# Hymba decoder layer on one core: values and decayed keys turned by VectorE and a DRAM scratch, transfers that add, one reciprocal-root operation in the layer norms, and a new order

## The chip, the cores and the metric

The kernel runs on one core of a Trainium2 chip. The core has a matrix engine (TensorE, PE in the profile, with its weight loads as PEld), VectorE (DVE), ScalarE (ACT), GpSimd (POOL) and SyncE (SP), which work in parallel, each through its own list of instructions in order, and which wait for each other by semaphores. SBUF is the memory on chip with 128 partitions, PSUM holds matmul results, DRAM lies outside and is reached by DMA transfers that an engine issues on its queue. The metric is the device time of one execution in microseconds (us), lower is better.

## The reference

One layer of a hybrid decoder, for a prompt of 512 tokens and, beside it, 8 decode tokens with their own past. All in float32, model width 1024.

```
h = x @ w_in                       # 3600 columns: qa ka va za ga | qb kb vb gb
# mixer A: gated linear attention, 4 heads, dk 64, dv 128, chunks of 64 tokens
S_t = diag(a_t) S_{t-1} + k_t^T v_t ;  o_t = q_t S_t        # a_t from za
o_a = rms_norm(o_a) * g
# mixer B: 8 heads of 64; three dilated windows (128,1) (512,4) (2048,16) with a
# relative-position bias, merged by their softmax denominators
mix = concat(o_a * silu(ga), o_b * silu(gb))
y   = mix @ w_out
out = layer_norm(alpha * x + y) * g + b                     # alpha = 2 ** 0.25
```

Outputs are the new rows of prompt and decode tokens, the GLA states (the prompt's last one, and s*a + k*v for each decode token), and the new key and value rows.

## The kernel before

**Tiling.** Everything is unrolled. The 512 prompt tokens and 8 decode tokens are projected in two halves (264 and 256 columns, the decode tokens in the first). Each fp32 product is three matmuls: weights and inputs are split into a high and a low part. `dense` (L804) holds the backbone of TensorE in the order of `ORDER` (L82): 21 groups of weight columns, qa0 to ga3, and then the output projection. For values (vb, va) the first half of the tokens comes out with features on partitions, and has to be turned to have tokens there; the second half is made in token layout at once.

**What sets the order.** `Plan` (L198) is a list scheduler that runs at build time. Each stage is a generator that yields operations, added with `add(gen, prio)`; the planner always takes the operation that can start first by its own cost table, the lower priority number first among equals, and issues it on its engine. Buffers come from `SLOTS` (SBUF, by tag) and `BANKS` (PSUM). So one engine's instruction order is fixed when the kernel is built, and every priority, slot count and cost moves it. All planned operations have the line of the helper that issues them, L380 in the profile.

**What is turned, and how.** `turn` (L730) copies a piece of 128 features by 256 tokens out of PSUM and turns it with two PE transposes (`ps_turn`); `vb_into` (L1219) uses it for the values of mixer B, f = 0 and 1 for each of v0 and v1. `gla_state` (L1019) turns the decayed keys `kd` (2 x 128 x 512) with eight PE transposes into `ps_kt` and copies them to `kt`, which the products `ps_kv` use. The output projection's pieces of tokens 0 to 255, in `out_turn` (L785), go another way for three of four column groups g: `blocks` (L740) turns 32 x 32 blocks on VectorE into `yw`, `store_blocks` writes `yw` to the DRAM scratch `ysc`, and `load_turned` loads it as `yx`, both on POOL's queue (`QUEUE`, y = "G"). `out_evac` (L1827) then adds `yx` to `y` with the residual's ALPHA, and takes `bn_stats`. The fourth group is turned by PE (`ps_yt`).

**The decode states.** `sample_state` (L1522) loads eight states `s` and their values `v`, multiplies by the decay on ScalarE, adds value times key on VectorE (16 operations each) and stores.

**Layer norm and end.** `norm` (L1874) centres each tile t of 128 tokens and scales it by a root from Ln and Exp with a Newton step (`rsqrt`, L410). Tile 3 ends the kernel: `early_mean` (L1698) prepares its mean, the last 256 columns are accumulated last in PSUM onto a seed that ScalarE writes, and `last_norm` (L1721) finishes: square and sum (`sq_y`), root, centre, three scalings and three stores. `ln_rows` (L1663) does the decode rows (`w_s`, `sums_s`), with two tiny products `ps_ms` and `ps_vs` that stand in PE's list among the last groups.

## Time and profile before

| | us |
|---|---|
| median of three runs | 276.61 (276.04 to 276.85) |
| the profiled execution | 276.23 |
| its span | 274.3 |
| busy: TensorE / VectorE / ScalarE / POOL | 264.2 / 220.6 / 157.9 / 64.0 |

The span reaches from the first to the last instruction of the profiled execution, which itself took 1.93 us more. The trace gives each instruction's start and duration; "<-" after idle time names what ended it. Names are the program's tiles, such as `ps_kt<-cf,kd` for a matmul into `ps_kt` from `cf` and `kd`. PE's own time is pipelined: a matmul of 256 columns is listed with 0.28 us, but the next one starts 0.12 after it.

### The profile page before, as it was taken

What the parts mean: (1) busy time and instruction counts of PE and PEld (TensorE: products, weight loads), DVE (VectorE), ACT (ScalarE), POOL (GpSimd) and SP (SyncE); (2) the same over time, 40 slices, a digit from 0 to 9 for tenths busy, and PEclk for the clock granted to TensorE, in tenths of its full rate; (3) what the DMA queues carried; (4) which work ended last, traced back from release to release, by engine and by line L of the source; (5) the groups of instructions that cost most, each with busy time, mean ns of one, the idle gap of its engine ahead of it and who ended that gap; (6) DMA issues with size and microseconds to landing.
All of it is one profiled execution on the core that took longest, in us unless ns stands there. A gap on an engine that the chain in (4) does not pass through costs nothing.

```text
span 274.3 us, 7448 instructions
## 1 busy us (share of the span) xinstructions
PE 264.2 (96%) x2869; PEld 248.9 (91%) x2869; DVE 220.6 (80%) x584; ACT 157.9 (58%) x478; POOL 64.0 (23%) x77
## 2 busy tenths in 40 slices
PE   8999999999799999999999999999999999999990
PEld 5999999899799999989998989999999999998890
DVE  5746789998989799988499954965989898448995
ACT  4727856565457676686464754735589975420221
POOL 3000000000576538220054435353200001330000
PEclk9999999999999999999999999999999999999997
DMA  6978948327959968737599999897952485896142
GB/s 212 342 192 196 301 130 226 81 76 210 307 172 278 236 206 273 194 84 203 153 223 279 282 219 272 217 206 162 244 159 76 114 290 144 228 282 192 58 171 81
DMA packets 62999, 54.67 MB, mean 199 GB/s; under 512 B 13933, under 2 KB 55059, under 8 KB 62965
## 3 DMA queue, kind: packets, MB, share of 16 engines
q1 hardware_dynamic: 61909, 52.18, 69.4%
q0 software_dynamic: 480, 1.57, 2.2%
q8 instruction: 22, 0.36, 0.5%
q10 hardware_dynamic: 576, 0.46, 0.5%
q14 instruction: 12, 0.10, 0.1%
HBM read 47.26 MB, written 7.73 MB: 200 GB/s over the span
## 4 chain that ended last, share of the span: by engine, by line
PE 80%; DMA 8%; DVE 6%; issue 2%; SPq 1%; POOL 0%; ACT 0%; DVEq 0%; POOLq 0%
PE ps_kb L380 9%; PE ps_ga L380 9%; PE ps_gb L380 9%; PE ps_qb L380 9%; PE ps_vb_f L380 4%; PE ps_va_f L380 4%; PE ps_vb L380 4%; PE ps_va L380 4%; PE ps_qa L380 4%; DMA ysc<-yw 4%; PE ps_yf L380 4%; DVE y L380 4%; PE ps_pv L380 3%; PE ps_s L380 3%; PE ps_ka L380 3%; DMA yx<-ysc 3%
## 5 line engine op out<-in xcount | busy, mean ns | idle before, releaser
L380 POOL TENSOR_TENSOR past<-past,qbc 128x256 f32<-128x256 f32 x32 | 29.0, 939 | 86.2 <-DMA qbc<-qsd 77.5
L380 POOL TENSOR_TENSOR vv<-vv,pb 128x256 f32<-128x256 f32 x32 | 26.8, 867 | 48.9 <-DMA pb<-psd_s 43.2
L380 ACT ACTIVATE pr<-pr,ms 128x128 f32<-128x128 f32 (+3 forms) x48 | 23.0, 493 | 7.8 <-DVE ms L380 7.8
L380 ACT COPY pt<-ps_pt 128x256 f32<-128x256 f32 (+1 forms) x29 | 9.8, 347 | 10.4 <-PE ps_pt L380 10.2
L380 DVE CUSTOM_DVE_ANT_0 pr<-ps_s,strip 128x128 f32<-128x128 f32 (+3 forms) x32 | 11.5, 407 | 3.9 <-PE ps_s L380 3.8
L380 ACT ACTIVATE sg<-sg 128x264 f32<-128x264 f32 (+1 forms) x32 | 13.7, 429 | 0.6
L380 PE MATMUL ps_ka<-xx,hi_ka 128*128 128x264 f32 (+1 forms) x64 | 12.2, 283 | 0.0
L380 POOL DMA_DIRECT2D ysc<-yw x3 | 2.5, 818 | 41.0 <-DVE yw L380 40.6
L380 PE MATMUL ps_pt<-cf,pr 128*128 128x128 f32 x56 | 11.3, 274 | 0.0
L380 DVE TENSOR_REDUCE lt<-past 128x8 f32<-128x512 f32 x16 | 10.5, 668 | 0.0
L380 PEld LDWEIGHTS ps_ka<-xx,hi_ka 128*128 128x128 f32 x64 | 9.9, 190 | 0.1
L380 DVE TENSOR_REDUCE o_pv<-vv 128x4 f32<-128x1024 f32 x8 | 9.7, 1206 | 0.0
L380 ACT ACTIVATE d<-d 128x512 f32<-128x512 f32 x11 | 6.6, 641 | 3.9 <-DVE d L380 3.8
L380 PE MATMUL ps_ka<-xx,lo_ka 128*128 128x264 f32 (+1 forms) x32 | 8.7, 283 | 0.0
L380 ACT ACTIVATE qh<-ps_qb 128x128 fp32r<-128x128 f32 x16 | 5.2, 438 | 5.9 <-PE ps_qb L380 5.8
L380 ACT COPY feat_y<-ps_yf 128x256 f32<-128x256 f32 x8 | 3.0, 373 | 8.9 <-PE ps_yf L380 8.9
L380 DVE TENSOR_TENSOR far<-tp,same 128x128 f32<-128x128 f32 (+1 forms) x16 | 8.1, 526 | 0.0
L380 DVE STREAM_TRANSPOSE yw<-feat_y 128x256 f32<-128x256 f32 x6 | 3.8, 640 | 4.8 <-ACT feat_y L380 4.7
L380 PE MATMUL ps_qa<-xx,hi_ka 128*128 128x264 f32 (+1 forms) x32 | 7.4, 304 | 0.1
L380 ACT CAST mhb<-gb 128x256 fp32r<-128x256 f32 x8 | 3.2, 405 | 7.2 <-DVE gb L380 7.2
L380 PEld LDWEIGHTS ps_pt<-cf,pr 128*128 128x128 f32 x56 | 6.9, 140 | 0.3 <-ACT hi_gb__2144 L380 0.2
L380 DVE TENSOR_TENSOR gb<-ps_gb,sg 128x256 f32<-128x256 f32 x8 | 3.4, 419 | 4.4 <-ACT sg L380 4.1
(574 smaller groups left out, 1079.1 us busy)
## 6 DMA issues: line engine op xcount, KB each, us to landing
past<-in_ck_dram SPq DMA_DIRECT2D x8, 512.0 KB, 4.7
vv<-in_cv_dram SPq DMA_DIRECT2D x8, 512.0 KB, 7.2
pb<-psd_s SPq DMA_DIRECT2D x16, 256.0 KB, 7.1
s<-in_state_dram SPq DMA_DIRECT2D x4, 512.0 KB
qbc<-qsd SPq DMA_DIRECT2D x8, 256.0 KB, 5.4
y<-in_xp_dram SPq DMA_DIRECT2D x4, 512.0 KB
x_raw<-in_xT_dram SPq DMA_DIRECT2D x6, 260.0 KB, 5.9
out_dram<-y SPq DMA_DIRECT2D x3, 512.0 KB
```

The lines of the kernel that those rows point to most:

```text
L380: getattr(eng.eng, op.fn)(*op.args, **op.kw)
```

## The change

1. Values of mixer B are turned by `blocks` on VectorE and a scratch `vsc` on SyncE's queue (new `rows_of`), the decayed keys by `blocks` and a scratch `ksc` on POOL's queue, in place of PE transposes.
2. Of the decode states, ScalarE multiplies both parts; the decayed state is stored plainly and the key times value is added to it in DRAM by an accumulating transfer.
3. The residual of tiles 0 and 1 is scaled by ALPHA on ScalarE after loading, and the projection's pieces are added to it by accumulating transfers from `ysc`; the statistics wait for each.
4. The layer norm roots are one Abs_reciprocal_sqrt with the Newton step as before; tile 2's mean and variance are made on ScalarE; in `last_norm` the centring stands ahead of the root; two of the last three stores go to SyncE's queue.
5. One slot of `w` more and one of `sv` less; `va1` ahead of `gb3`; nearly all priorities renumbered.

```diff
-SLOTS = dict(g=23, w=7, r=3, sv=5, pt=2, ...
+SLOTS = dict(g=23, w=8, r=3, sv=4, pt=2, ...
-QUEUE = dict(y="G")
+QUEUE = dict(y="G", v="D", k="G")
-ORDER = "... gb1 va0 gb2 gb3 va1 ga0 ga1 ga2 ga3".split()
+ORDER = "... gb1 va0 gb2 va1 gb3 ga0 ga1 ga2 ga3".split()
...
         if between:
-            yield S.activation(o, x, AF.Ln, scale=scale, bias=ln_eps)
+            yield S.activation(o, x, AF.Abs_reciprocal_sqrt, scale=scale, bias=ln_eps)
             yield V.tensor_scalar(half, x, -0.5 * scale, -0.5 * eps, op0=ALU.mult, op1=ALU.add)
-            yield S.activation(o, o, AF.Exp, scale=-0.5)
...
+    def rows_of(g, f, ps):
+        yield from make(f"vbw{g}", Need("g", f"vbw{g}", [P, 2, 2, P])) if f == 0 else iter((At(f"vbw{g}"),))
+        w = B[f"vbw{g}"]
+        feat = yield Need("t1", "feat", [P, GW])
+        yield copy(feat, ps[:, :GW])
+        free(ps)
+        yield blocks(w[:, :, f], feat)
+        free(feat)
+        if f:
+            yield store_blocks(queue["v"], vsc[g], w.rearrange("p t f c -> p (t f) c"))
+            free(w)
+            yield load_turned(queue["v"], B[f"v{g}"][:, :2, :].rearrange("p t (k j) -> p (t k) j", j=32), vsc[g])
...
+        kx = yield Need("g", "kx", [P, 2, NP])
+        for m in range(2):
+            yield blocks(kx[:, m].rearrange("p (c t) -> p c t", c=TT), kd[:, m])
+        yield store_blocks(queue["k"], ksc, kx.rearrange("p m (c t) -> p (m c) t", c=TT))
         kt = yield Need("g", "kt", [P, 2, TT, P])
-        for m in range(2):
-            ps = yield bank("t", "ps_kt")
-            for c in range(TT):
-                yield T.transpose(ps[:, c * P:c * P + P], kd[:, m, c * P:c * P + P], ident)
-            yield copy(kt[:, m].rearrange("p c t -> p (c t)"), ps)
+        yield load_turned(queue["k"], kt.rearrange("p m c (a j) -> p (m c a) j", j=32), ksc)
...
-            ps, raw = yield from turn(ps)
-            free(raw)
-            yield copy(B[f"v{i}"][:, :2, f * P:f * P + P], ps[:, :GW].rearrange("p (t c) -> p t c", t=2))
+            yield from rows_of(i, f, ps)
...
-                    yield S.mul(s4[:, bb, m, :], s4[:, bb, m, :], a_s[:, m, bi:bi + 1])
-                    yield V.scalar_tensor_tensor(s4[:, bb, m, :], v4[:, bb, m, :], ka_s[:, m, bi:bi + 1], s4[:, bb, m, :],
-                                                 op0=ALU.mult, op1=ALU.add)
+            for x, scale in ((s4, a_s), (v4, ka_s)):
...
+                yield D.dma_start(to, x) if scale is a_s else G.dma_start(to, x, accum_op=ALU.add)
...
+        if t < 2:
+            yield S.mul(y, y, ALPHA)
...
         yield At("early_centre")
-        yield S.activation(root, ss, AF.Ln, scale=1.0 / DM, bias=q)
+        yield V.scalar_tensor_tensor(y[:, x], ps, mean, B["gamma"][:, x], op0=ALU.subtract, op1=ALU.mult)
+        yield S.activation(root, ss, AF.Abs_reciprocal_sqrt, scale=1.0 / DM, bias=q)
         yield V.tensor_scalar(half, ss, -0.5 / DM, dev, op0=ALU.mult, op1=ALU.add)
-        yield V.scalar_tensor_tensor(y[:, x], ps, mean, B["gamma"][:, x], op0=ALU.subtract, op1=ALU.mult)
-        yield S.activation(root, root, AF.Exp, scale=-0.5)
...
-            yield (D if i == 1 else S).dma_start(y_p[t * P:t * P + P, c], y[:, c])
+            yield (D if i else S).dma_start(y_p[t * P:t * P + P, c], y[:, c])
...
-            yx = yield Need("g", f"yx{g}", [P, 2, GW])
-            yield load_turned(queue["y"], yx.rearrange("p t (k j) -> p (t k) j", j=32), ysc[g])
             for t in range(2):
-                add(out_evac(t, g, yx[:, t]), 2)
+                yield At(f"y{t}")
+                yield G.dma_start(B["y", t][:, g * GW:g * GW + GW].rearrange("p (k j) -> p k j", j=32),
+                                  ysc[g][8 * t:8 * t + 8].rearrange("k p j -> p k j"), accum_op=ALU.add)
+                add(out_stats(t, g, 1), 9.2)
...
+            sq = yield Need("r", f"sq{t}", [P, DM])
+            yield S.activation(sq, y, AF.Identity, accum_out=mv[:, 0:1])
+            yield S.mul(mean, mv[:, 0:1], -1.0 / DM)
+            yield S.activation(sq, y, AF.Square, bias=mean, accum_out=mv[:, 1:2])
```

What this does to the instruction lists is shown at three places. The first is TensorE's list before, inside the third part of the values group vb0 (`ps_vb0_3`, from weights `hi0_vb0`, `lo0_vb0` and inputs `xx`), with `ps_pt21` a transpose of the attention and `ps_kt` the turned keys:

```order
L380 MATMUL ps_vb0_3_1538<-hi0_vb0__912,xx0_133 128x256
L380 MATMUL ps_pt21_1524<-cf_66,pr20_1331 128x128 x2
L380 MATMUL ps_vb0_3_1538<-hi0_vb0__912,xx2_215 128x256
L380 MATMUL ps_vb0_3_1538<-lo0_vb0__991,xx2_215 128x256
L380 MATMUL ps_vb0_3_1538<-hi0_vb0__912,xx2_216 128x256
L380 MATMUL ps_kt_1532<-cf_66,kd_1408 128x128 x4
```

The same part of the same group in the changed kernel, on TensorE:

```order
L382 MATMUL ps_vb0_3_1539<-hi0_vb0__909,xx0_132 128x256
L382 MATMUL ps_vb0_3_1539<-lo0_vb0__910,xx0_132 128x256
L382 MATMUL ps_vb0_3_1539<-hi0_vb0__909,xx0_133 128x256
L382 MATMUL ps_vb0_3_1539<-hi0_vb0__909,xx2_215 128x256
L382 MATMUL ps_vb0_3_1539<-lo0_vb0__910,xx2_215 128x256
L382 MATMUL ps_vb0_3_1539<-hi0_vb0__909,xx2_216 128x256
```

The four transposes of the keys are gone from the list, as are the second four and those of the values, and nothing takes their place.

The second is the end of POOL's list, which issues the scratch transfers of the projection's pieces; before:

```order
L380 DMA ysc0_95<-yw0_3878 128x4x128
L380 DMA ysc1_96<-yw1_3921 128x4x128
L380 DMA yx0_3918<-ysc0_95 128x16x32
L380 DMA ysc2_97<-yw2_3957 128x4x128
L380 DMA yx1_3953<-ysc1_96 128x16x32
L380 DMA yx2_4004<-ysc2_97 128x16x32
```

In the changed kernel, where `out_3_dram<-v40` and `<-v41` are the state adds and `y0`, `y1` the tiles that are added to:

```order
L382 DMA out_3_dram<-v40_3486 128x8x128
L382 DMA ysc0_95<-yw0_3875 128x4x128
L382 DMA ysc1_96<-yw1_3910 128x4x128
L382 DMA y0_3706<-ysc0_95 128x8x32
L382 DMA y1_3708<-ysc0_95 128x8x32
L382 DMA y0_3706<-ysc1_96 128x8x32
L382 DMA y1_3708<-ysc1_96 128x8x32
L382 DMA ysc2_97<-yw2_3952 128x4x128
L382 DMA out_3_dram<-v41_3813 128x8x128
L382 DMA y0_3706<-ysc2_97 128x8x32
L382 DMA y1_3708<-ysc2_97 128x8x32
```

The third store stood behind one load and stands behind four adds now, and a state add has come between it and the two adds that need it.

The third is VectorE's list in the last groups of the output projection, up to the copy of `ps_ms` and the first work that needs the third scratch; before:

```order
L380 BN_STATS stats1_3729<-y1_3728 128x6
L380 SCALAR_TENSOR_TENSOR y2_4042<-y2_4042,ps_y20_4079 128x512
L380 BN_STATS stats2_4043<-y2_4042 128x6 x2
L380 COPY sums_s_85<-ps_ms_4118 64x1
L380 TENSOR_SCALAR w_s_3730<-w_s_3730,sums_s_85 64x128
L380 SCALAR_TENSOR_TENSOR y0_3726<-y0_3726,yx2_4004 128x256
L380 SCALAR_TENSOR_TENSOR y1_3728<-y1_3728,yx2_4004 128x256
```

In the changed kernel the two statistics at the top are those that wait for the adds from the second scratch:

```order
L382 BN_STATS stats0_3707<-y0_3706 128x6
L382 BN_STATS stats1_3709<-y1_3708 128x6
L382 TENSOR_TENSOR y0_3706<-y0_3706,ps_yt3_4033 128x256
L382 TENSOR_TENSOR y1_3708<-y1_3708,ps_yt3_4033 128x256
L382 BN_STATS stats0_3707<-y0_3706 128x6
L382 BN_STATS stats1_3709<-y1_3708 128x6
L382 SCALAR_TENSOR_TENSOR w_s_3710<-w_s_3710,ps_ys_4076 64x128
L382 TENSOR_REDUCE sums_s_85<-w_s_3710 64x1
L382 SCALAR_TENSOR_TENSOR y2_4035<-y2_4035,ps_y20_4068 128x512
L382 COPY sums_s_85<-ps_ms_4105 64x1
```

The sums that `ps_ms` is made from stand behind those statistics; the additions of `yx` and tile 2's statistics are gone.

More of the change, by code (lines that the diff above doesn't have):

```diff
@@ L96, in __init__ @@
             self.writes.append(kw["accum_out"])
+        if "accum_op" in kw:
+            self.reads = self.reads + [aps[0]]
         if fn == "tensor_tensor_reduce":
@@ L408, in cst, with rsqrt @@
         return const.tile(shape, dt, name=name)
-    def rsqrt(o, x, scale, eps, between=None):
+    def rsqrt(o, x, scale, eps, between=None, late=False):
         n = size(x)
@@ L424, in rsqrt @@
             yield V.tensor_scalar(x, x, scale, eps, op0=ALU.mult, op1=ALU.add)
-            yield S.activation(o, x, AF.Ln)
-            yield S.activation(o, o, AF.Exp, scale=-0.5)
+            if late:
+                yield S.activation(o, x, AF.Abs_reciprocal_sqrt)
+            else:
+                yield S.activation(o, x, AF.Ln)
+                yield S.activation(o, o, AF.Exp, scale=-0.5)
             yield V.tensor_tensor(t, o, o, op=ALU.mult)
@@ L750, in load_turned @@
         return q.dma_start(out, sc.rearrange("k p j -> p k j"))
+    def rows_of(g, f, ps):
[10 more added lines that the diff above has]
+            yield load_turned(queue["v"], B[f"v{g}"][:, :2, :].rearrange("p t (k j) -> p (t k) j", j=32), vsc[g])
+            for _ in range(2):
+                mark(f"vb{g}")
     def sample_rows(x, rows):
@@ L832, in dense @@
         free(zw, *xraw)
-        add(gate_decay(pz), 19.1)
+        add(gate_decay(pz), 41.3)
         yield from make("ka", Need("g", "ka", [P, 2, NP]), 3)
@@ L843, in dense @@
             add(residual(t), 10.3)
-        add(residual_sample(), 19.7)
+        add(residual_sample(), 40.8)
         units = [(g, f) for g in range(4) for f in range(2)]
@@ L960, in gla_levels @@
             if li % 2:
-                add(gla_level(made), 46.7)
+                add(gla_level(made), 62.4)
                 made = []
@@ L1121, in gla_out @@
         for i in range(2):
-            add(gla_head(u, i, ps, po), 26 + u + i / 2)
+            add(gla_head(u, i, ps, po), 51.1 + u + i / 2)
     def gla_head(u, j, ps, po):
@@ L1163, in evac @@
             if n == "k":
-                add(keys_out(ps, m, u), 9.7)
+                add(keys_out(ps, m, u), 56.4)
             else:
@@ L1772, in out_first @@
             yield from out_half(g, f, p, range(4, KT))
-            add(out_turn(g, f, p), 0.3)
+            add(out_turn(g, f, p), 10.7)
     def out_half(g, f, ps, ks):
@@ L1830, in out_evac, with out_stats @@
         c = slice(g * GW, g * GW + size(ps))
-        yield V.scalar_tensor_tensor(y[:, c], y[:, c], ALPHA, ps, op0=ALU.mult, op1=ALU.add)
+        if t < 2:
+            yield V.tensor_tensor(y[:, c], y[:, c], ps, op=ALU.add)
+        else:
+            yield V.scalar_tensor_tensor(y[:, c], y[:, c], ALPHA, ps, op0=ALU.mult, op1=ALU.add)
         free(ps)
-        for i in range(g, g + size(ps) // GW):
-            yield V.bn_stats(st[:, i, :], y[:, i * GW:i * GW + GW])
+        yield from out_stats(t, g, size(ps) // GW)
+    def out_stats(t, g, n):
+        y, st = B["y", t], B["stats", t]
+        for i in range(g, g + n):
+            if t not in (2,):
+                yield V.bn_stats(st[:, i, :], y[:, i * GW:i * GW + GW])
             mark(f"y{t}_done")
@@ L1867, in residual_sample @@
         free(ps, avg)
-        yield from rsqrt(rstd, sums[:, 1:2], 1.0, LN_EPS)
+        yield from rsqrt(rstd, sums[:, 1:2], 1.0, LN_EPS, late=True)
         yield V.scalar_tensor_tensor(y, y, rstd, gamma, op0=ALU.mult, op1=ALU.mult)
```

99 lines of the change are left out of this document (51 added, 48 removed).

## The prediction

> **What bounds the kernel now.** I read the page's header first: busy time of each engine, the row of tenths, the software queue and the chain that ended last.
>
> ```profile
> span 274.3 us, 7448 instructions
> PE 264.2 (96%) x2869; PEld 248.9 (91%) x2869; DVE 220.6 (80%) x584; ACT 157.9 (58%) x478; POOL 64.0 (23%) x77
> PE   8999999999799999999999999999999999999990
> q0 software_dynamic: 480, 1.57, 2.2%
> PE 80%; DMA 8%; DVE 6%; issue 2%; SPq 1%; POOL 0%; ACT 0%; DVEq 0%; POOLq 0%
> ```
>
> TensorE is busy in 39 of 40 slices, so what it no longer does comes off the end, unless another chain ends as late. The next view cuts the span into stretches: start and end, length, then the busy time of PE, PEld, DVE, ACT and POOL, the granted clock, the DMA share and GB/s.
>
> ```profile
> 60.00:100.00 40.00, 38.53 (x583) 36.46 (x583) 35.69 (x92) 25.12 (x72) 18.72 (x20) 1.00 0.78 220
> 245.00:267.60 22.60, 22.60 (x126) 19.21 (x124) 20.49 (x60) 3.73 (x20) 1.15 (x1) 1.00 0.46 152
> 267.60:274.30 6.70, 0.01 (x1) 0.00 (x0) 3.35 (x9) 1.06 (x4) 0.00 (x0) 0.76 0.24 83
> ```
>
> PE has no gap from 245 on, and VectorE is nearly as full there (20.49 of 22.60). After 267.6 only the last layer norm and its stores are left. So two chains meet at the end: PE's, and the one that feeds VectorE with the projection pieces of tokens 0 to 255, which go through a DRAM scratch on the POOL queue. The timeline of POOL (start, duration, what) shows the second; the last two lines are the chain's, where a duration reaches to the landing.
>
> ```profile
> 232.41 0.93 POOL L380 DMA_DIRECT2D ysc<-yw  x1 [38.61 <-DVE yw L380]
> 238.04 1.17 POOL L380 DMA_DIRECT2D yx<-ysc  x1 [1.97 <-DMA ysc<-yw]
> 239.67 0.76 POOL L380 DMA_DIRECT2D ysc<-yw  x1 [0.47 <-DVE s L380]
> 240.42 1.16 POOL L380 DMA_DIRECT2D yx<-ysc  x1
> 239.67 5.38 DMA ysc<-yw
> 245.59 7.09 DMA yx<-ysc
> 252.70 0.76 DVE L380 SCALAR_TENSOR_TENSOR y<-y,yx 128x256 f32<-128x256 f32 x2 [0.53 <-DMA yx<-ysc]
> 253.37 0.75 DVE L380 BATCH_NORM_STATS2 stats<-y 128x6 f32<-128x256 f32 x2
> 254.52 2.47 DVE L380 SCALAR_TENSOR_TENSOR y<-y,mv,gamma 128x1024 f32<-128x1024 f32 x2
> ```
>
> The last of these loads is in at 252.70, and VectorE then works until 268.35 without a real pause, 15.65 us. PE's last matmul ends at 267.61 (below). The two are within 1 us, so a gain needs both. The profiled execution took 276.23 us, 1.93 more than its span; the sum is made against it. The median of the three runs is 276.61, 0.38 more.
>
> **PE's transposes.** Two edits take work from PE: the values of tokens 0 to 255 (four pieces, two transposes each) and the decayed keys (eight) are turned by VectorE and a DRAM scratch. The chain view gives start, duration and count:
>
> ```profile
> 85.05 0.22 PE ps_turn L380 x2
> 90.57 0.44 PE ps_kt L380 x4
> 93.26 0.44 PE ps_kt L380 x4
> 54.40 0.69 issue
> 73.62 1.47 issue
> ```
>
> Removed: 2 x 0.44 + 4 x 0.22 = **1.76 us** in a stretch without slack. The order of the changed kernel has no other matmul fewer or more. In their place VectorE gets block transposes:
>
> ```profile
> L380 DVE STREAM_TRANSPOSE yw<-feat_y 128x256 f32<-128x256 f32 x6 | 3.8, 640 | 4.8 <-ACT feat_y L380 4.7
> 93.87 1.72 DVE L380 TENSOR_TENSOR lo_kb__1590<-raw_kb__1078,hi_kb__1395 128x1024 fp32r<-128x1024 f32 x1
> 103.30 0.28 PE L380 MATMUL ps_kb<-xx,lo_kb__1590 128*128 128x264 f32 x1
> L380 PEld LDWEIGHTS ps_kv<-va,kt x64: 129/133/133, 189.1 to 194.1; 64*64 64x64 f32 x64
> ```
>
> Four of 0.64 for the values and two of twice the size, 1.28 each, for the keys: 5.1 us, of which 3.8 fall into the stretch 60 to 100, whose 35.69 become 39.5 of 40. That is the tightest place. What hides it is the lead of the weight splits: lo_kb__1590 is ready at 95.59 and first used at 103.30. The lead of 7.7 falls to some 4; without it each further us is one of PE. The turned keys are needed at 189.1, about 95 us after they were made, so a store and a load of 5 to 7 us each vanish there. They also put a wait on POOL (the load stands behind its store, ahead of the fifth past product), and POOL has time: 64.0 of 274.3 busy. The turned values come one scratch trip later, and the new order has moved the products that read them behind the next projection groups. Cost taken: 0, bounds 0 to 2 us. The two "issue" pauses (0.69 and 1.47, PE waiting for nothing that shows, behind bursts of small matmuls) stay, move or go: -2.2 to +1.5, taken as 0.
>
> **The sample state.** Sixteen VectorE operations go and sixteen ScalarE ones come:
>
> ```profile
> L380 DVE SCALAR_TENSOR_TENSOR s<-v,ka_s,s 128x128 f32<-128x128 f32 x16 | 5.0, 344 | 0.8 <-ACT s L380 0.8
> L380 ACT ACTIVATE s<-s,a_s 128x128 f32<-128x128 f32 x16 | 6.0, 408 | 0.0
> ```
>
> VectorE gains 5.0 us, ScalarE pays 16 x 0.408 = 6.5; it is busy 157.9 of 274.3, and no end waits for it there. The two new 512 KB adds into the output matter only as company on the POOL queue.
>
> **The y pieces.** Here lies the risk. Three loads of 256 KB become six adding transfers of 128 KB on the same queue, and POOL's order is new: four adds now stand ahead of the third store, and the second state add ahead of the last two. The six VectorE adds go.
>
> ```profile
> L380 DVE SCALAR_TENSOR_TENSOR y<-y,yx x6: 417/419/425, 244.3 to 253.0; 128x256 f32<-128x256 f32 x6
> DMA to landing us min/median/max: 5.8/6.2/7.1
> L380 PE MATMUL ps_ms<-sums_s,avg x2: 167/182/198, 250.8 to 250.9; 66*66 66x1 f32 x2
> ```
>
> Everything before comes 1.76 earlier, so the first adds are issued at 238.04 - 1.76 = 236.3, then about 1.0 apart (between 0.76 and 1.17 a DMA), the fourth at 239.3. The third store follows at 240.3 and lands after 5.38, at 245.7; 0.5 later the last two adds, at 246.2 and 247.2 (the state add is issued in that wait). With the median of 6.2 the last add lands at **L = 253.4**, 0.7 later than the load did. No row shows an adding transfer. From below: the queue's packets took 2.2% of 274.3 = 6.0 us for six transfers, 1.0 per 256 KB, so 0.5 per add if adding is free. From above: a store and a load behind each other, 5.38 + 7.09 = 12.5 us for one. I take the price of a load, since the rows of one are the nearest; the other end is the first rival.
>
> After L VectorE has less to do: of the 15.65, 0.76 (adds of y) and 0.75 (the statistics of tile 2, now on ScalarE) and 0.26 (their aggregate, by the same step) go, leaving 13.9; and tile 0's own add lands 1.0 ahead of tile 1's, so part of its 1.24 (half of 2.47) stands before L. I take 13.3. The chain then ends at 253.4 + 13.3 = 266.7 instead of 268.35. Two places of PE must also not wait: ps_ms, now 249.0, stands behind statistics that wait for the fourth add (239.3 + 6.2 = 245.5, and behind it five or six operations of about 0.42, some 2.3 us: 247.8, so 1.2 us of slack), and the last unit, whose seed stands on ScalarE behind the root chains of tiles 0 to 2 (it holds until L is about 255.7).
>
> A rule speaks against this. The Trainium skill, "Collectives: The Full Stack", section "The bandwidth ceiling: the fold count and why AG ≠ RS ≠ AR", says that a DMA that adds is slower not for the arithmetic but because it reads two sources on one ring, so that it moves about half as much. No run here shows it yet; by it an add would take 1.0 of the queue instead of 0.5, which the 1.0 between issues still covers, and the sum would be about 0.5 higher.
>
> **The layer norm roots.** One operation replaces Ln and Exp, and it needs another ACT table.
>
> ```profile
> 267.33 0.28 PE L380 MATMUL ps_y<-hi_wo__3598,mla 128*128 128x256 f32 x1
> 268.25 0.29 ACT L380 ACTIVATE tail<-tail,tail 128x1 f32<-128x1 f32 x1
> 268.57 0.20 ACT L380 ACTIVATE tail<-tail 128x1 f32<-128x1 f32 x1
> 268.65 0.47 DVE L380 SCALAR_TENSOR_TENSOR y<-ps_y,tail,gamma 128x256 f32<-128x256 f32 x1
> 270.10 1.41 ACTq L380 DMA_DIRECT2D out_dram<-y  x2
> 270.76 0.33 SPq L380 DMA_DIRECT2D out_dram<-y  x1
> L597 ACT ACT_TABLE_LOAD x1 | 1.3, 1283 | 1.7 <-PEq L2021 1.7
> 252.26 0.31 ACT L380 ACTIVATE sq_s<-w_s 64x128 f32<-64x128 f32 x1 [7.40 <-DVE w_s L380]
> ```
>
> At the end the Exp's step goes (0.20 and a gap of 0.03), and the centring of 0.47 runs beside the square instead of behind it; about 0.3 us. The last store, the second of two on ScalarE's queue (1.41 / 2 = 0.7), goes to SyncE's (0.33): another 0.3. Together **0.6**, between 0.2 and 1.0. The new table load stands behind sq_s, where ScalarE had waited 7.40 us and has only 3.73 us of work in 22.6. Its 1.283 is hidden if what comes next waits for L, as it does.
>
> The Trainium skill, "ScalarE: Activation LUTs", section "What ACT_TABLE_LOAD costs", adds a drain of about 1380 ns to the load of 1283 ns; the load agrees with the row, the drain no run here shows. By it 2.66 us would still lie inside that wait, and the sum is the same.
>
> **The sum.** PE: last matmul 267.61 - 1.76 = 265.85; behind it came 276.23 - 267.61 = 8.62, now 8.0: 273.9. VectorE: 266.7, and behind it 276.23 - 268.35 = 7.88, now 7.3: 274.0. The later is 274.0 against 276.23; the median would stand up to 0.38 higher, and I say **274.2**.
>
> **Rivals.**
> (a) *Adds that clog the queue: slower.* If an add occupies the queue for t us, then above t = 1.0 (the distance of the issues) the third store stands behind four of them and the last add behind one more: L = 253.4 + 0.5 + 5 (t - 1). The kernel is slower than before once L + 13.3 + 7.3 passes 276.23, L = 255.6, t about 1.35. At t = 2 L is 258.9 and the time **279.5**; the last unit of PE waits too, inside the same chain. For it: reading, adding and writing 128-byte rows in SBUF is nowhere in the trace, and the order puts the third store behind the adds. Against it: 0.5 us plain is 2.7 times below the turning point.
> (b) *The gain is spent elsewhere: no change.* A full VectorE at 60 to 100, a longer pause after the small matmuls, or the order's new places cost PE 1.5 to 2.5 us in the middle: **276**. For it: 39.5 of 40. Against: the lead of 7.7 us, and 5.0 us that VectorE is spared elsewhere.
> (c) *The pauses vanish with the new order*: 274.2 - 2.2 = **272.0**, if L also comes early.
> (d) *It does not do what it says*, the transposes gone but the y chain not shorter (L as late as 255): within 0.3% of before; I count it with (b).
>
> **How the numbers follow.** Forecast 0.58, (a) 0.23, (b) with (d) 0.14, (c) 0.05. Faster by over 0.3% (0.83 us, about what a measurement of this kernel can tell from no change): 0.58 + 0.05 = 0.63; same 0.14; slower 0.23. The forecast's own range is 272.8 to 275.6: terms of -0.4 and +0.4 in the tail, -1 for pauses, +1 for L. The range for 8 in 10 goes down to (c)'s 272.0 and up to 279.0, most of (a); beyond it lie about half of (a) and half of (c), 0.14.
>
> **What would show it.** Right: no ps_kt, PE's last matmul near 265.9; the last add of y landing at 253 to 254.5; the statistics of tile 0 not waiting past 253; a table load inside ScalarE's wait before the roots; the final stores in at 272 or earlier. Wrong: VectorE idle before statistics on an adding transfer past 255, PE idle before ps_ms or the last unit (case a); PE idle between 75 and 130 on a split of weights or on "issue" (case b); adds that take more than 1.35 us of the software queue each.

## The result: slower, and the profile after

The changed kernel takes **280.60 us** (median of four runs, 280.52 to 281.31) against 276.73 for the kernel before beside it: a ratio of **1.0139** (95% interval 1.0107 to 1.0171). The forecast was 274.2, with a range that ended at 279.0. So both the sign and the range were wrong, and the rival that had named this outcome, the adds that clog the queue, came in. The profiled execution took 281.31 us, 5.08 more than that of before.

The page's header, in the same order as before: busy times, the 40 slices of TensorE and of its granted clock, the software queue, and one group of instructions with what ended the idle time ahead of it.

```profile
span 279.5 us, 7413 instructions
PE 264.9 (95%) x2853; PEld 248.6 (89%) x2853; DVE 228.0 (82%) x580; ACT 159.4 (57%) x474; POOL 74.3 (27%) x84
PE   8999999999999989999999999999989999986990
PEclk9999999999999999999999999999999999997996
q0 software_dynamic: 8848, 3.67, 10.4%
L382 DVE BATCH_NORM_STATS2 stats<-y 128x6 f32<-128x256 f32 x11 | 4.5, 419 | 13.9 <-DMA y<-ysc 13.9
```

TensorE has 16 instructions fewer, as forecast, but is busy 0.7 us longer. Two slices near the end show holes: PE falls to 8 tenths in slice 36 and to 6 in slice 37, and the clock to 7 tenths in slice 37. VectorE stood idle 13.9 us in all ahead of the statistics of `y`, waiting for adding transfers. And the software queue has 8848 packets where it had 480, in 10.4% of the span instead of 2.2%.

The views by stretch (start and end, length, busy time of PE, PEld, DVE, ACT and POOL, granted clock, DMA share, GB/s):

```profile
60.00:100.00 40.00, 39.62 (x590) 38.18 (x589) 39.91 (x92) 23.53 (x71) 17.98 (x23) 1.00 0.80 236
245.00:267.60 22.60, 19.29 (x86) 15.38 (x84) 13.82 (x32) 7.57 (x22) 4.27 (x3) 0.92 0.92 139
250.50:253.80 3.30, 0.00 (x0) 0.02 (x1) 2.61 (x9) 0.00 (x0) 1.35 (x2) 1.00 1.27 174
253.80:257.80 4.00, 3.99 (x12) 3.21 (x13) 1.14 (x3) 1.69 (x3) 1.77 (x2) 0.58 1.20 74
```

From 245 on PE was full before (22.60 of 22.60) and VectorE nearly (20.49). Now both have holes: PE does nothing at all for 3.3 us, and then works for 4 us at a granted clock of 0.58.

The timelines of POOL, VectorE and PE (start, duration, engine, what; in brackets the idle time ahead and what ended it) give the chain behind these holes. The last two rows sum up the six adds: the duration of an issue on POOL (ns; shortest, median, longest) with the first and the last start, and the time from issue to landing.

```profile
236.13 3.21 POOL L382 DMA_DIRECT2D y<-ysc  x2
240.65 3.11 POOL L382 DMA_DIRECT2D y<-ysc  x2 [1.31 <-DMA ysc<-yw]
242.42 2.14 POOL L382 DMA_DIRECT2D ysc<-yw  x1
243.20 2.95 POOL L382 DMA_DIRECT2D out_dram<-v  x1
252.45 3.12 POOL L382 DMA_DIRECT2D y<-ysc  x2 [6.30 <-DMA ysc<-yw]
251.48 0.43 DVE L382 BATCH_NORM_STATS2 stats<-y 128x6 f32<-128x256 f32 x1 [0.66 <-DMA y<-ysc]
258.11 0.43 DVE L382 BATCH_NORM_STATS2 stats<-y 128x6 f32<-128x256 f32 x1 [3.13 <-DMA y<-ysc]
253.81 0.25 PE L382 MATMUL ps_ms<-sums_s,avg 66*66 66x1 f32 x2 [3.31 <-issue]
L382 POOL DMA_DIRECT2D y<-ysc x6: 1535/1928/2283, 236.1 to 253.3; - x6
DMA to landing us min/median/max: 5.3/9.8/12.3
```

The third store is issued at 242.42 and is in only at 252.45, ten us later, where a store took 5.38 before; behind it the last two adds begin. The first of them, tile 0's, lands at **L = 258.11**, and VectorE works on from there; the second, issued at 253.3 and 5.3 us under way, lands at about 258.6, before VectorE asks for it. The forecast for the last add was 253.4. The fourth add lands at 251.48 instead of 245.5, and since the sums for `ps_ms` stand behind its statistics in VectorE's list, PE waits 3.31 us there. The trace calls that wait "issue"; the release is read from VectorE's list, which reaches the sums (253.43 to 253.71) just ahead of it.

### The profile page after: what moved, and what is told of

It is laid out like the page before. It is cut to its first block, busy times and chain, and to the rows that moved or that the text cites. A ratio compares the mean times of both kernels' runs of the same rounds, so it can differ in the third digit from the quotient of the medians.

```text
span 279.5 us, 7413 instructions
## 1 busy us (share of the span) xinstructions
PE 264.9 (95%) x2853; PEld 248.6 (89%) x2853; DVE 228.0 (82%) x580; ACT 159.4 (57%) x474; POOL 74.3 (27%) x84
## 3 DMA queue, kind: packets, MB, share of 16 engines
q0 software_dynamic: 8848, 3.67, 10.4%
## 5 line engine op out<-in xcount | busy, mean ns | idle before, releaser
L382 POOL TENSOR_TENSOR past<-past,qbc 128x256 f32<-128x256 f32 x32 | 26.4, 859 | 82.3 <-DMA qbc<-qsd 80.0
L382 POOL TENSOR_TENSOR vv<-vv,pb 128x256 f32<-128x256 f32 x32 | 27.8, 897 | 56.9 <-DVE ms L382 20.3
L382 ACT ACTIVATE pr<-pr,ms 128x128 f32<-128x128 f32 (+3 forms) x48 | 22.7, 491 | 12.6 <-DVE ms L382 12.6
L382 DVE BATCH_NORM_STATS2 stats<-y 128x6 f32<-128x256 f32 x11 | 4.5, 419 | 13.9 <-DMA y<-ysc 13.9
L382 PE MATMUL ps_pt<-cf,pr 128*128 128x128 f32 x56 | 10.9, 276 | 1.0 <-ACT pt L382 0.6
L382 POOL DMA_DIRECT2D y<-ysc x6 | 9.4, 1910 | 7.6 <-DMA ysc<-yw 7.6
L382 ACT COPY pt<-ps_pt 128x256 f32<-128x256 f32 (+1 forms) x23 | 7.6, 348 | 5.7 <-PE ps_pt L382 5.6
L382 POOL DMA_DIRECT2D out_dram<-v x2 | 4.6, 2278 | 21.2 <-ACT v L382 21.2
L382 DVE TENSOR_SCALAR pr<-pr,ms 128x320 f32<-128x320 f32 (+3 forms) x16 | 7.9, 497 | 0.2
L382 DVE TENSOR_TENSOR far<-tp,same 128x128 f32<-128x128 f32 (+1 forms) x16 | 7.1, 475 | 0.0
L382 ACT CAST xx<-x_raw 128x520 fp32r<-128x520 f32 (+2 forms) x10 | 5.3, 540 | 3.0 <-DMA x_raw<-in_xT_dram 2.9
```

The lines of the kernel that those rows point to most:

```text
L382: getattr(eng.eng, op.fn)(*op.args, **op.kw)
```

## The experiments

All ratios are to the kernel before, measured on the same chip beside the run, with 95% intervals.

**Which of the adds costs it.** Three kernels put parts of the change back. `e1_y_plain` loads the projection's pieces plainly, three loads of 256 KB, and adds them on VectorE; all else is the changed kernel:

```diff
-            for t in range(2):
-                yield At(f"y{t}")
-                yield G.dma_start(B["y", t][...], ysc[g][...], accum_op=ALU.add)
-                add(out_stats(t, g, 1), 9.2)
+            yx = yield Need("g", f"yx{g}", [P, 2, GW])
+            yield load_turned(queue["y"], yx..., ysc[g])
+            for t in range(2):
+                add(out_evac(t, g, yx[:, t]), 9.2)
```

> The changed kernel with the projection pieces of tiles 0 and 1 loaded plainly from their scratch and added by VectorE, as before; the state adds stay on POOL's queue. Theory A (the six y adds clog the software queue): the load of the third piece lands at about 253 instead of 258.4, TensorE does not wait before ps_ms, its clock does not drop, its last matmul ends at about 267.6 and the time is 275.5 to 277. Rival B (the new order in the middle of the kernel sets the time): no more than 1 us comes back, 279.5 or more. Rival C (the state add of 512 KB on the same queue is as bad): the load lands at 255 or later, 278 to 279.

`e2_state_plain` has the adds for `y`, and the decode states as before (ScalarE's multiply, VectorE's multiply and add, one store):

> The changed kernel with the decode states added by VectorE and stored once, as before; the six y adds stay. Theory A: the queue still has six adds of about 2.3 us, the last lands near 255 because the third store now stands behind two of them fewer and the 4.2 us of the state add are gone: 277 to 278.5, still slower than before. Rival C (the state add is what delays the last y adds): the last add lands before 254 and the time is 276.5 or less. Rival B: 280, no change.

`e3_no_adds` has both edits:

> The changed kernel without any adding transfer: turned values and keys, new roots, new priorities stay. Theory A: 275 to 276, bounded by TensorE, whose list up to the last ps_yf ends at 244.3 in both kernels; so the 1.76 us of transposes stay lost in the middle and only the end gains. Rival B: 279 or more. Rival D (the adds were the only loss, the transposes' gain comes through without them): 274 or less.

| | median us | ratio |
|---|---|---|
| e1, y plain | 275.24 | 0.9952 (0.9932 to 0.9972) |
| e2, state plain | 280.48 | 1.0145 (1.0102 to 1.0189) |
| e3, neither adds | 276.36 | 0.9985 (0.9960 to 1.0011) |

The adds into `y` cost 5.2 us with the state's adds beside them (1.0139 - 0.9952 = 1.87% of 276.7) and 4.4 without (1.0145 - 0.9985 = 1.60%); they are the whole loss and more. Taking the state's adds out, which gives VectorE its sixteen operations back, gains nothing that shows; with plain loads of `y` they even seem to gain about 0.9 us (0.9952 against 0.9985, though the two intervals overlap a little). e2 missed its expectation of 277 to 278.5. In its trace the last add lands at 256.06, some 2.5 us earlier than in the changed kernel, but PE still waits 2.06 us at `ps_ms` and the clock is 0.57 for 4 us behind it; what keeps its time at 280.5 was not separated. The rest of the change is worth half a per cent, as e1 shows. In e1 the queue and the first work that needs the third scratch are:

```profile
q0 software_dynamic: 2848, 3.67, 6.7%
252.63 0.76 DVE L382 TENSOR_TENSOR y<-y,yx 128x256 f32<-128x256 f32 x2 [1.33 <-DMA yx<-ysc]
245.00:267.60 22.60, 21.94 (x123) 18.66 (x121) 19.86 (x57) 8.14 (x25) 1.17 (x1) 1.00 0.53 146
```

L is 252.63, the clock 1.00, and PE has 21.94 of 22.60 again.

**What of it is the adding, what the six transfers in that order.** `e9_six_loads` keeps the six transfers of 128 KB and their places in POOL's list, but loads and lets VectorE add:

```diff
-                yield G.dma_start(B["y", t][...], ysc[g][8 * t:8 * t + 8]..., accum_op=ALU.add)
-                add(out_stats(t, g, 1), 9.2)
+                yx = yield Need("g", f"yx{g}{t}", [P, GW])
+                yield G.dma_start(yx..., ysc[g][8 * t:8 * t + 8]...)
+                add(out_evac(t, g, yx), 9.2)
```

> The changed kernel with the same eleven transfers in the same order on POOL's queue, but the six of y are plain loads of 128 KB into six tiles, and VectorE adds them. If the adding itself holds the queue (1024 packets of 128 bytes, about 2 us an add): the last pair lands near 253 and the time is 275 to 276.5, as with three loads. If six transfers with the third store behind four of them are the cause, whatever they do: 279 or more.

`e5_rows_1k` adds in the same six places, but each transfer has 128 rows of 1 KB in DRAM and SBUF instead of 1024 pieces of 128 bytes. It leaves out the turn of these pieces, so tiles 0 and 1 get other values:

```diff
-                yield G.dma_start(B["y", t][...].rearrange("p (k j) -> p k j", j=32),
-                                  ysc[g][8 * t:8 * t + 8].rearrange("k p j -> p k j"), accum_op=ALU.add)
+                yield G.dma_start(B["y", t][...],
+                                  ysc[g][8 * t:8 * t + 8].rearrange("k (a b) j -> (k a) (b j)", b=8), accum_op=ALU.add)
```

> The changed kernel with the same six adds of 128 KB, but each reads its half of the scratch as 128 rows of 1 KB and not as 1024 pieces of 128 bytes: the pieces are added without their turn, so tiles 0 and 1 of the output are not the reference's. If an add costs by the packet (36 ns for 128 bytes and 64 ns for 512 in the changed kernel's queue, so some 100 ns for 1 KB, 0.8 us of 16 engines instead of 2.3), the adds no longer clog the queue, the last lands near 253 and the time is 274.5 to 276.5. If it costs by the byte (two sources read), nothing changes: 280.

e9 took 277.87, ratio 1.0035 (1.0011 to 1.0060); e5 278.58, ratio 1.0053 (1.0018 to 1.0088). So of the 1.87% that separates the changed kernel from e1, 0.83% (2.3 us) is there with plain loads in the six places, and 1.04% (2.9 us) comes from adding; with long rows adding costs about half a us over e9, inside both intervals. Both kernels lie between the two times that had been expected of them: the adding and the six places each make a part of the loss. The software queue of e9, of e5, and the first work behind the third scratch in e9:

```profile
q0 software_dynamic: 2896, 3.67, 6.6%
q0 software_dynamic: 3472, 3.67, 7.5%
254.45 0.43 DVE L382 TENSOR_TENSOR y<-y,yx 128x256 f32<-128x256 f32 x1 [4.59 <-DMA yx<-ysc]
```

These rows price an add. The bytes are the same 3.67 MB in all three kernels; the packets are 8848 with adds and 2896 with loads, and the difference of 5952 is 6 x (1024 - 32): an adding transfer makes **one packet of every 128-byte piece**, a plain one 32 for the whole 128 KB. e5 fits it with one packet for each row, 576 = 6 x (128 - 32) more than e9. In time, 10.4% of 279.5 is 29.1 us and 6.6% of 276.0 is 18.2: 10.9 us for six, 1.8 each on top of the 0.5 that the rows of before gave for a plain one. So the packets of an add take **2.3 us** of the 16 engines' time, not 0.5. In rows of 1 KB it is (7.5% of 275.8 = 20.7, less 18.2) / 6 = 0.4 on top, 0.9 in all. These are estimates from sums of packet times, and not distances between landings: the first four adds of the changed kernel land at 247.78, 249.34, 250.40 and 251.48, the first 11.6 us after its issue and the others 1.1 to 1.6 apart.

The Trainium skill's rule that was weighed in the prediction ("Collectives: The Full Stack", section "The bandwidth ceiling: the fold count and why AG ≠ RS ≠ AR", half the rate because an add reads two sources) is stated there for the reduce step of a ring collective. Applied to these transfers it agrees with the 1 KB rows, 1.8 times the plain price, and not with the 128-byte rows of this change, 4.6 times. The two differ in the length of the pieces, and so in their packets, 128 against 1024 an add.

**Each kind of add in the old order.** Two kernels put one kind into the kernel before, with its own priorities. `e10_y_adds_in_before` has the ALPHA on ScalarE and the six adds:

> The kernel before with nothing but the six y adds (and the scaling of tiles 0 and 1 on ScalarE). If the adds cost by themselves: 4 to 5.5 us more than before, 281 to 282. If they hurt only in the new order, or because the state adds share the queue: 277 to 279.

`e11_state_adds_in_before` has the plain store and the adding transfer for the decode states:

> The kernel before with nothing but the state adds (16 operations of VectorE go to ScalarE, two adds of 512 KB on POOL's queue). e1_y_plain against e3_no_adds gives 1.1 us for them; if that comes from VectorE's 5 us in the last stage: 275.4 to 276. If they delay the y loads on the queue: 277 or more.

e10 took 283.45, ratio 1.0222 (1.0186 to 1.0258): 6.1 us for the adds into `y`, in an order not made for them. e11 took 280.46, ratio 1.0098 (1.0061 to 1.0136): here the state's adds cost 2.7 us, where in the new order they cost nothing that shows. The queue of e10 with PE's longest wait in it, and the first work behind the third scratch in e11:

```profile
q0 software_dynamic: 6480, 1.57, 5.8%
PE ps_ms L382 <- DVE sums_s L382: 5.2, 1, 5.2
256.81 0.76 DVE L382 SCALAR_TENSOR_TENSOR y<-y,yx 128x256 f32<-128x256 f32 x2 [0.52 <-DMA yx<-ysc]
```

e10 gives the price a second time: 5.8% of 282.3 is 16.4 us against 6.0 before, so six adds take 10.4 us more than three loads of 256 KB, 1.7 each. It also loses at `ps_ms`, 5.2 us. In e11 a state add of 512 KB stands ahead of the pieces' stores, and L moves from 252.70 to 256.81. Not all of that is the queue's: in e11 PE's last matmul into `ps_yf` already starts 2.1 us later than before (246.21 against 244.09).

**Is the wait at ps_ms the loss?** `e6_ms_ahead` makes the statistics of the added pieces wait until the decode sums are through, so that `ps_ms` no longer stands behind an add; PE's list is the same:

```diff
         yield V.tensor_reduce(sums[:, 0:1], y, axis=AX.X, op=ALU.add)
+        mark("w_sum")
...
-                add(out_stats(t, g, 1), 9.2)
+                add(out_stats(t, g, 1, True), 9.2)      # begins with: yield At("w_sum")
```

> The changed kernel, all adds as they are, but the decode rows' sums stand ahead of the statistics that wait for adds on VectorE, so TensorE no longer waits 3.3 us before ps_ms and its clock should not fall to half. If the chain behind the last add (some 15 us of VectorE without a pause) sets the end by itself, the time stays at 279.5 to 280.6. If TensorE's wait and its slow clock set it, 5 us come back: 276.

It took 279.40, ratio 1.0099 (1.0062 to 1.0136). The wait is gone, and only 1.1 us of some 5 came back (0.40% of 276.8). The profiled execution took 282.01, 2.6 more than that median: behind a wait of 1.75 at `ps_oa` the clock was 0.57 for 4 us, and PE's last matmul into `ps_yf` starts 2.1 later than in the changed kernel (246.13 against 244.06). So its times can be compared only with each other. The rows are PE's longest wait after the warm-up, its last matmul, and VectorE's centring of 768 columns:

```profile
PE ps_oa L382 <- ACT oa L382: 1.8, 1, 1.8
270.70 0.28 PE L382 MATMUL ps_y<-hi_wo__3535,mla 128*128 128x256 f32 x1
273.05 1.01 DVE L382 SCALAR_TENSOR_TENSOR y<-y,tail,gamma 128x768 f32<-128x768 f32 x1
```

PE is through at 270.98, 2.07 us before VectorE begins that centring; in the changed kernel the two lie within 0.4 (272.68 and 272.27). A wait on the path was removed, and a second path of nearly the same length, VectorE's behind the last add, stood behind it.

**The state add ahead of the last pair.** `e8_state_last` is e1 with the second state add issued after the last load of `y`:

```diff
+                if i and scale is ka_s:
+                    yield At("yx_in", 3)
                 yield D.dma_start(to, x) if scale is a_s else G.dma_start(to, x, accum_op=ALU.add)
```

> e1_y_plain with the second 512 KB state add issued after the last load of y instead of ahead of it. The state add holds the queue for 4 us ahead of that load (its data runs from 246.9 to 250.9, the load's from 251.3), so the load lands some 3 us earlier, near 249.5; TensorE's end does not change, so the time is 274.4 to 275.3. If the state add runs past the end of the stores, it is longer: 276 or more.

275.33, ratio 0.9941 (0.9911 to 0.9971). It beats both kernels, and so does e1; the two can't be told apart by their times, though L came at 251.14 in e8's profile (249.5 had been expected).

**What the transposes are worth.** `e4_turns_only` makes only the turns of values and keys in the kernel before, with its old priorities. `e7_y_plain_pe_turns` is e1 with the turns back on PE, at the new priorities:

> The kernel before with nothing but the values and the decayed keys turned by VectorE and DRAM, old priorities. If the transposes are a gain by themselves: 1.8 us less than before, 275.0. If new waits of TensorE eat it (the pauses move, VectorE is full between 60 and 100): between 276 and 277.5.

> e1_y_plain with values and decayed keys turned by TensorE again, under the new priorities. If taking the 1.76 us of transposes off TensorE is worth its size there: 277.0. If the new waits behind the scratch trips eat it: 275.2 to 276.

Both missed: e4 took 290.68, ratio 1.0535 (1.0466 to 1.0604), and e7 284.47, ratio 1.0213 (1.0146 to 1.0280). By e4 alone the edit would cost 14 us, by e7 against e1 (2.6%) it would gain 7. What they show is the order: a list scheduler given other work with priorities made for something else sends operations to other places. In e4, PE's two longest waits at `ps_pt`, and the stretch from 117 to 124, which has the longer one in it and the shorter one ahead of it:

```profile
PE ps_pt L380 <- DVE pt L380: 4.3, 1, 4.3
PE ps_pt L380 <- ACT pt L380: 2.1, 1, 2.1
117.00:124.00 7.00, 3.63 (x50) 2.89 (x51) 4.99 (x15) 1.25 (x4) 4.62 (x6) 0.51 0.08 23
```

So a third kernel left the order alone. `e13_dead_transposes` is e8 with 16 transposes whose results nobody reads, four at the start of each unit of the vb groups, and all other instructions in their places:

```diff
+                if k == 0 and g.name[:2] == "vb":
+                    for c in range(4):
+                        nc.tensor.transpose(ps[:, c * P:c * P + P], ident, ident)
```

> e8_state_last with sixteen transposes put back on TensorE as dead work (four of 128x128 into the fresh bank of each first-half values piece, overwritten at once), every list otherwise word for word the same. They take 16 x 0.11 = 1.76 us. If TensorE sets the time there, as e8's TensorE end (266.1) and its span (272.9) say: 1.5 to 1.8 us more than e8, 276.9 to 277.1, about the time of before; then the transposes are worth their size and the rest of e8 gains nothing. If there is slack: 275.3 to 276.

276.70, ratio 1.0008 (0.9986 to 1.0029), against e8's 0.9941: 0.67% or **1.85 us**, good to about 1 us by the two intervals. With the order fixed, PE's transposes are worth about their size, 16 x 0.11 = 1.76. In the two profiles PE's last matmul ends 1.26 later (267.33 against 266.07), since the wait at `ps_oa` falls from 1.6 to 0.6.

**The roots.** `e12_y_plain_ln_exp` is e1 with Ln and Exp in place of the one operation in all three spots:

```diff
-            yield S.activation(o, x, AF.Abs_reciprocal_sqrt, scale=scale, bias=ln_eps)
+            yield S.activation(o, x, AF.Ln, scale=scale, bias=ln_eps)
...
+            yield S.activation(o, o, AF.Exp, scale=-0.5)
```

> e1_y_plain with Ln and Exp for the roots as before and no second table load. If one root operation saves 0.3 us at the end: 275.5 to 275.8. If VectorE's own list (the 768-wide centring before the last piece) sets the end, so that the root does not matter: 275.2, no change.

275.16, ratio 0.9931 (0.9900 to 0.9962), where e1 has 0.9952. The new root is worth nothing that these runs can see.

**PE's new wait at ps_oa.** `e14_last_product_late` is e8 with GpSimd's last product of the decode attention held back by a one-column copy on VectorE, until mark `oa_done1` of mixer A's outputs has passed:

```diff
+        if bi == NB - 1:
+            yield At("oa_done1")
+            yield V.tensor_copy(pf[:, 0:1], pf[:, 0:1])
```

> e8_state_last with the last of the sample value products on POOL (four operations of 128x256) held back until the first half of the linear attention's output is scaled, by a one-column copy on VectorE that it depends on. In e8 VectorE's small operations of that output's Newton step take 0.6 us each instead of 0.16 while that product runs (198.6 to 201.4), and TensorE waits 1.6 us before ps_oa. If POOL's work beside them is the cause: that wait falls below 0.5 and the time to 274 or 274.5. If the wait has another cause, it stays: 275.3; later work on VectorE may then lose as much.

276.56, ratio 1.0010 (0.9987 to 1.0033): no gain, and 0.7% more than e8. The first three rows are of e8 (GpSimd's product, one of VectorE's small operations under it, PE's wait), the last of e14:

```profile
198.64 2.80 POOL L382 TENSOR_TENSOR vv<-vv,pb 128x256 f32<-128x256 f32 x4 [6.27 <-DVE oa L382]
199.43 0.66 DVE L382 TENSOR_TENSOR newton<-newton,ssq 128x4 f32<-128x4 f32 x1
PE ps_oa L382 <- ACT oa L382: 1.6, 1, 1.6
200.50 0.16 DVE L382 TENSOR_TENSOR newton<-newton,ssq 128x4 f32<-128x4 f32 x1
```

The small operations go from 0.66 to 0.16 and the wait at `ps_oa` vanishes. The profiled execution is the longest of e14's twelve (278.03), and PE is 1.9 us later in it than in e8 at the first matmul with `hi_ga__2719` (191.5 against 189.6), but level at the last with `hi_ga__3006` (205.6 in both). So the cause of this wait was found, but the kernel got other waits, of which the longest after the warm-up is 1.2 us at `ps_ms`.

## Why the prediction was wrong

**The step that failed** is the sentence "I take the price of a load, since the rows of one are the nearest". The packets of an add of 1024 pieces take 2.3 us of the queue instead of 0.5, above the turning point of 1.35 that the first rival had named. The third store, which stands behind four adds, then waits for the queue, and the last pair behind the store. The store came in 6.75 us late (252.45 against 245.7). Of this 4.65 is its time on the queue (10.03 against 5.38). The other 2.1 is its issue (242.42 against 240.3): the third add, and with it all that stands behind it, waits for the second store until 240.65, a wait that the sum didn't have. What the prediction lacked was the count of packets: 480 for six transfers and 1.57 MB stood in its own row, so a plain transfer goes in packets of some 3 KB, while the form of the adds (128 rows of eight 32-element pieces) stood in the program. Whether an add can be packed as well was the open question, and it was answered by taking the nearest row without a bound by pieces.

**The sum by the first rival**, with t = 2.3, gives L = 253.4 + 0.5 + 5 x 1.3 = 260.4 and 281.0; the profile has 281.31, but by two errors against each other. The last add lands at about 258.6, 1.8 earlier than by this sum (258.11, from which VectorE works on, is 2.3 earlier). Behind L the prediction took 13.3 + 7.3 = 20.6 us, and it is 22.7 from 258.6, and 23.2 from 258.11 (281.31 - 258.11), as before (276.23 - 252.70 = 23.5) and in e1 and e9 (22.9 and 23.4). So even adds at the price of loads would have given about 253.4 + 22.7 = 276.1 to 253.4 + 23.2 = 276.6, no change. e9, with plain loads in the same six places, had L at 254.45 and took 277.87. The two terms behind L that were mis-sized:

- *VectorE spared 2.35 us after L*: from L to the centring of 768 columns it took 267.34 - 252.70 = 14.64 before and 272.27 - 258.11 = 14.16 now, 0.5 less. The first three rows show it: VectorE's work (the third busy time of a row) is 13.61 instead of 14.54, 0.93 less, but it stands idle for 0.55 instead of 0.10.
- *The tail's 0.6*: nothing. In the other rows, VectorE's list holds the last centring until 273.33, behind the centring of 768 columns:

```profile
252.70:267.34 14.64, 14.64 (x90) 12.91 (x88) 14.54 (x42) 3.32 (x18) 0.00 (x0) 1.00 0.26 107
258.11:272.27 14.16, 14.16 (x86) 12.50 (x85) 13.61 (x36) 5.89 (x19) 0.00 (x0) 1.00 0.28 113
267.34 1.01 DVE L380 SCALAR_TENSOR_TENSOR y<-y,tail,gamma 128x768 f32<-128x768 f32 x1
269.04 0.51 DVE L380 TENSOR_SCALAR tail<-tail,tail 128x1 f32<-128x1 f32 x2
272.40 0.28 PE L382 MATMUL ps_y<-hi_wo__3535,mla 128*128 128x256 f32 x1
272.27 1.01 DVE L382 SCALAR_TENSOR_TENSOR y<-y,tail,gamma 128x768 f32<-128x768 f32 x1
273.33 0.48 DVE L382 SCALAR_TENSOR_TENSOR y<-ps_y,tail,gamma 128x256 f32<-128x256 f32 x1
273.73 0.83 DVE L382 TENSOR_SCALAR tail<-tail,tail 128x1 f32<-128x1 f32 x3
```

PE's last matmul ends at 272.68 and the execution 8.63 later; before it was 267.61 and 8.62. The last centring starts 1.06 us behind the start of the one of 768 columns, where it was 1.31 (268.65 - 267.34), 0.25 less; but three tiny operations (0.83) follow where two (0.51) did. The store that moved to SyncE's queue gained nothing either: from VectorE's last operation to the end of the span it is 3.36 us (276.14 to 279.5), and was 3.18 (271.12 to 274.3). e12 shows from the other side that the new root brings nothing.

**The wait at ps_ms** was named with 1.2 us of slack; the fourth add was 6 us late, and the slack became a wait of 3.31. PE's last matmul moved from 267.61 to 272.68, 5.07 later: 3.31 of waiting, and in the 4 us at a clock of 0.58 another 1.7 (4.00 x 0.42), 5.0 in all. e6 shows that this isn't the loss by itself: without the wait PE is through 2.07 us before VectorE's chain gets to the centring of 768 columns.

**PE's 1.76** was right as a size (e13: 1.85, good to about 1), but is not seen in the changed kernel. PE reaches the end of the last group of features no earlier than before; below the same matmul in before and after:

```profile
244.09 0.29 PE L380 MATMUL ps_yf<-mla,hi_wo__3846 128*128 128x264 f32 x1
244.06 0.29 PE L382 MATMUL ps_yf<-mla,hi_wo__3797 128*128 128x264 f32 x1
```

The two pauses of before (1.47 and 0.69) are gone, which the prediction left open, and other waits have come, from PE's waits in the changed kernel:

```profile
PE ps_oa L382 <- ACT oa L382: 1.2, 1, 1.2
PE ps_kb L382 <- ACT qk L382: 0.9, 1, 0.9
PE ps_pt L382 <- ACT pt L382: 0.6, 1, 0.6
PE ps_pt L382 <- ACT pr L382: 0.4, 1, 0.4
PE ps_ort L382 <- DVE o_r L382: 0.3, 1, 0.3
```

They make 3.4 us. With 1.76 and 2.16 saved, some 0.5 remains that I can't place in one execution. So the cost in the middle, taken as 0 with a bound of 2, was of the size that the second rival gave it. The stretch from 60 to 100 was forecast with VectorE at 39.5 of 40 and has 39.91; whether the waits at `ps_kb` and `ps_pt`, behind ScalarE, come from there, no run here tells.

**What was right**: no transposes of keys and values; the table load inside ScalarE's wait (the rows stand below); the state's adds as mere company in this order (e2 against the changed kernel); and the mechanism of the first rival with its place. Its price was close by two errors, and its turning point was too high: e9 with an estimated 0.5 us and e5 with 0.9 are already slower than before (1.0035 and 1.0053). e8, where nothing clogs the queue, comes nearest to the forecast: PE's last matmul ends at 266.07 (forecast 265.85) and the profiled execution took 274.70; what separates it from 274.0 is mostly the tail, 8.63 us behind PE's end where 8.0 was forecast.

From ScalarE's timeline of the changed kernel, the new table load and the first root:

```profile
255.49 1.28 ACT L382 ACT_TABLE_LOAD   x1
258.87 0.29 ACT L382 ACTIVATE rstd<-mv,ln_eps 128x1 f32<-128x1 f32 x1 [2.09 <-DVE mv L382]
```

The load costs what the row of before gave. The drain that the Trainium skill adds to it ("ScalarE: Activation LUTs", section "What ACT_TABLE_LOAD costs") can't be told here, since ScalarE stood idle for 2.09 us behind the load in any case, waiting for VectorE.

**The chances and the range** followed the failed step. The first rival got 0.23, though for an operation that no row shows its bounds were 0.5 and 12.5 and the turning point lay at 1.35; and the range was cut at 279.0, below that rival's own price at t = 2; the text calls what lies below that bound "most of (a)" and reckons with half.

## What to carry to other kernels

Before a transfer is made to add, count its contiguous pieces: here every piece of 128 bytes became a packet, so that an add of 1024 pieces took the packet time of 4.6 plain transfers, while one of 128 rows took that of 1.8. Ask next what stands behind it on its queue, and what small product stands behind its consumer on an engine in order; a rival whose turning point lies between the bounds of an unknown price deserves a chance by that distance, not by the nearest row. And where two chains end within 1 us of each other, a gain must be shown in both, and a list scheduler's part can be priced only with the order held still, as with dead transposes.

## What the runs showed of the hardware

- **Packets of an adding transfer**: one for each 128-byte piece (8848 packets against 2896), by estimate from the packet times 2.3 us of the 16 engines for 128 KB; 0.9 in rows of 1 KB; 0.5 plain.
- **The clock falls after some of PE's waits, and their length doesn't decide it**: it was 0.58 of full speed over 4 us behind 3.31 us in the changed kernel, and 0.57 behind 2.06 in e2 and behind 1.75 in e6 (at `ps_oa`). It stayed at 1.00 behind 2.25 in e5 and behind 3.31 in e7, both at `ps_ms`. In e4, with waits of 2.1 and 4.3 us close to each other, it was 0.51 over 7 us. The rows are of e2, e6, e5 and e7, each from the end of the wait or just behind it:

```profile
251.90:255.90 4.00, 4.00 (x12) 3.24 (x13) 1.50 (x6) 0.89 (x3) 0.13 (x1) 0.57 1.26 88
204.55:208.55 4.00, 4.00 (x95) 3.29 (x96) 3.97 (x10) 2.68 (x10) 0.00 (x0) 0.57 0.37 111
251.60:255.60 4.00, 4.00 (x20) 3.29 (x21) 3.05 (x8) 2.77 (x7) 0.25 (x1) 1.00 0.55 74
258.80:262.80 4.00, 4.00 (x19) 3.27 (x20) 4.00 (x13) 1.86 (x10) 0.00 (x0) 1.00 0.01 4
```

  The Trainium skill, "TensorE: Matmul & The Clock Gate", section "What's actually happening", says that the clock goes to one half after an idle window of some 3.4 us, which runs free of the work. The size of the fall agrees roughly, the length does not: 1.75 and 2.06 us were enough, and 3.31 in e7 was not. What else decides, no run here shows.
- **Small VectorE operations beside GpSimd's product**: 128x4 in 0.56 to 0.66 us instead of 0.16, shown from both sides by e8 and e14. In e1 it is seen within one execution: 0.16 just before GpSimd's product begins at 200.18, and 0.68 right after.
